# Gate's second half: one feature group of each pair of blocks by seven products of sums, and up's partial sums seeded in PSUM by ScalarE

## The chip, the cores and the metric

The kernel runs on one core of a Trainium2 chip. The metric is the device time of one execution in microseconds (us). TensorE (PE) does the matrix products, VectorE (DVE) and ScalarE (ACT) work on SBUF and PSUM, GpSimd (POOL) does little here, and SyncE (SP) issues nearly all DMA transfers.

## The reference

One transformer layer over 256 tokens with 2048 features, in float32: modulated input, a combined q/k/v projection, two kinds of attention over the tokens and 256 context tokens, an output projection, a gated residual and LayerNorm, and then a feed-forward part with the same residual rule. The change touches the feed-forward part alone:

```
def swiglu(u, w_gate, w_up, w_down):
    return (jax.nn.silu(u @ w_gate) * (u @ w_up)) @ w_down
```

Here u is 256 x 2048, w_gate and w_up are 2048 x 5632, and w_down is 5632 x 2048.

## The kernel before

**Precision by three products.** TensorE multiplies float32 rounded to a shorter form (F32R). Each operand is split into a rounded part hi and a remainder lo, and each product is three matmuls, hi x hi, hi x lo and lo x hi (`mm3`, L331 to L333). For the weights, ScalarE makes hi by a cast (L321) and VectorE lo by a subtraction (L322), on pieces of 128 x 1024 (`split_raw`). There are four buffers each for hi and lo (`HL_BUFS`), so the splits can run at most four pieces ahead of the matmuls, and four raw buffers of 1 MB (`RAW_BUFS`) into which SP loads the weights. For the tokens, u is turned (features on the partitions) and split once into `u2h` and `u2l` by `z_part`.

**Blocks and groups.** The 5632 columns of gate and up are cut into eleven blocks f of 512, the 2048 features into four groups g of 512 (four tiles k of 128 each). `project(accs, w_, f, g, ...)` loads and splits the weights of one group and one block and adds its product for both halves of the tokens (t = 0, 1) into two PSUM banks, 24 matmuls of 128x512 in all.

**Two halves.** Blocks 0 to 9 (`SPLIT_F` = 10) are worked in two halves, because the later features of u are ready late. The first half does one group (blocks 0 to 2) or two groups (blocks 3 to 9) and copies the sums to SBUF tiles `spills[f]` (gate in [0], up in [1]; L1568). The second half, a loop over f, does the remaining groups in new PSUM banks, and `activate` adds the spilled sums on VectorE (L1493, L1494), applies Silu on ScalarE (L1496) and multiplies (L1497). Block 10 is done whole.

**Turning.** The product h of a block is turned for the down projection: a 32x32 transpose on VectorE (`squares`, L1507), a trip through DRAM by SP's queue (`put`, `get`), and a split into `hTh` and `hTl` (`place`). `turn()` counts groups, and emits these steps some groups later.

**Order.** The attention part is put in order by a planner of the kernel's own. The feed-forward part is not: its instructions are ordered at compile time by a list scheduler, which keeps the program order as a priority, but puts an instruction earlier where its inputs are ready and its engine is free. At run time each engine follows that order.

**Banks and shared buffers.** PSUM has eight banks, four in a pool "acc" and four in a pool "wk". In SBUF, the tag "lgb" is one buffer, used by the sums of a modulation vector and then by `residual_base`, and "t2k" is four buffers, used by `z_part` and, from block 10 on, by the turning.

Of the kernel before, what the change touches and what calls it, by code (L numbers as in the profile page):

```python
# [13 lines left out]
F32 = mybir.dt.float32  # L14
F32R = mybir.dt.float32r
# [3 lines left out]
AF = mybir.ActivationFunctionType  # L19
ALU = mybir.AluOpType  # L20
# [27 lines left out]
SLACK = 2500  # L48
AHEAD = 14
EARLY_G = 2  # L50
ONE_F = 3
SPLIT_F = 10
LAG_S = 2
# [203 lines left out]
def dit_layer(ctx: ExitStack, tc: tile.TileContext, x, c, cx, c_ctx, w_ada, b_ada, w_in, q_norm_g,  # L257
# [68 lines left out]
    def split(hi, lo, src):  # L326
        nc.scalar.copy(hi, src)
        nc.vector.tensor_tensor(lo, src, hi.bitcast(F32), op=ALU.subtract)

    def mm3(ps, xh, xl, w, first, last, seeded=False):  # L330
        nc.tensor.matmul(ps, lhsT=xh, rhs=w[0], start=first, stop=False, skip_group_check=seeded)  # L331
        nc.tensor.matmul(ps, lhsT=xh, rhs=w[1], start=False, stop=False, skip_group_check=seeded)  # L332
        nc.tensor.matmul(ps, lhsT=xl, rhs=w[0], start=False, stop=last, skip_group_check=seeded)  # L333
# [1124 lines left out]
    def z_part(kk):  # L1458
        ps = wk_bank()
        for j in range(2):  # L1460
            for t in range(NT):
                nc.tensor.transpose(ps[:, (j * 2 + t) * P : (j * 2 + t + 1) * P],
                                    xt[:, t, (kk + j) * P : (kk + j + 1) * P], ident)
        uf = pb.tile([P, 2, SEQ], F32, tag="t2k", name="uf2", bufs=4)
# [4 lines left out]
        nc.vector.tensor_tensor(u2l[:, kk : kk + 2, :], uf, u2h[:, kk : kk + 2, :].bitcast(F32), op=ALU.subtract)  # L1469
# [12 lines left out]
    def project(accs, w_, f, g, first, last):  # L1482
        w = load_split(w_, g * 4, f * NB)
        for j in range(4):
            k = g * 4 + j
            for t in range(NT):
                mm3(accs[t], u2h[:, k, t * P : (t + 1) * P], u2l[:, k, t * P : (t + 1) * P], w[j], k == first, k == last)

    def activate(f, t, gate, up, hh):

        if f < SPLIT_F:
            sg, su = spills[f][0][:, t, :], spills[f][1][:, t, :]
            nc.vector.tensor_add(sg, sg, gate)  # L1493
            nc.vector.tensor_add(su, su, up)  # L1494
            gate, up = sg, su
        nc.scalar.activation(hh, gate, AF.Silu)  # L1496
        nc.vector.tensor_mul(hh, up, hh)  # L1497

# [28 lines left out]
    def flip_steps(f, gu):  # L1527

        if f < SPLIT_F:
            hh, hx = ([c[:, t, :] for t in range(NT)] for c in spills[f])  # L1530
        else:
            hh, hx = ([t2k(name) for t in range(NT)] for name in ("hh", "hx"))
        for t in range(NT):
            activate(f, t, gu[0][t], gu[1][t], hh[t])
# [87 lines left out]
    z_part(6)  # L1622
    cutoff = len(first_half) - 2
    run(merge(first_half[2 * ONE_F : cutoff], side))
    for kk in range(EARLY_G * 4, KD, 2):
        z_part(kk)
    run(first_half[cutoff:])
    flips = []

# [5 lines left out]
            flips.remove(e)  # L1635
            e[1]()

    for f in range(FFN // NB):
        if 5 <= f < 9:
            residual_base(f - 5)  # L1640
# [168 lines left out]
```

## Time and profile before

| | |
|---|---|
| median of 3 runs | 1134.47 us (1132.88 to 1136.02) |
| the profiled execution | 1133.72 us |
| its span, first to last instruction | 1131.9 us |
| PE, DVE, ACT busy, share of the span | 98%, 75%, 49% |
| granted TensorE clock | 0.996 |
| the feed-forward's second half, blocks 0 to 9 | about 585 to 835 us |

"Busy" is the time in which an engine has an instruction at work; matmuls overlap, so the distance between two starts is the better measure of TensorE. A line such as "L322 DVE TENSOR_TENSOR lo<-raw,hi" names the source line, the engine, the operation, what it writes and what it reads. In a list in order of time, the first number is the start in us, the second the duration (of a run of equal instructions where "x2" or more stands behind it), and the bracket is the idle time before it and what ended that. "PEld" is the loading of TensorE's stationary operand.

### The profile page before, as it was taken

How to read it: one execution, taken by the hardware profiler on the slowest of the kernel's cores; microseconds unless marked ns; L12 is line 12 of the kernel's file. 1: busy time of each engine (PE TensorE's matmuls, PEld its weight loads, DVE VectorE, ACT ScalarE, POOL GpSimd, SP SyncE). 2: the span in 40 equal slices, each digit the busy share in tenths (PEclk: the TensorE clock that was granted, in tenths of full speed). 3: DMA queues.
4: the chain of work that ended last, by engine and by line, in shares of the span. 5: the costliest groups of instructions: out<-in, count | busy, mean ns of one | idle time of the engine just before them, and what ended most of it. 6: DMA issues, size and time to landing. Idle time of an engine off the chain costs nothing.

```text
span 1131.9 us, 14059 instructions
## 1 busy us (share of the span) xinstructions
PE 1112.0 (98%) x5255; PEld 891.9 (79%) x5255; DVE 843.7 (75%) x1070; ACT 551.7 (49%) x795; POOL 43.2 (4%) x82
## 2 busy tenths in 40 slices
PE   8999999999999999999999999999999999999995
PEld 6767688778877787888888888888888888888884
DVE  5853489999999898777767566776766787686576
ACT  3341464878684255444464444444444344343442
POOL 1000050110200000010000000000000000000000
PEclk9999999999999999999999999999999999999998
DMA  9999999777999688999876776777677898887541
GB/s 316 395 389 354 405 362 359 250 253 225 362 339 385 241 301 308 343 312 317 303 234 216 240 237 223 230 242 258 213 265 241 272 370 303 312 303 260 187 148 74
DMA packets 178317, 321.26 MB, mean 284 GB/s; under 512 B 8732, under 2 KB 43196, under 8 KB 175943
## 3 DMA queue, kind: packets, MB, share of 16 engines
q1 hardware_dynamic: 177528, 320.03, 80.8%
q8 instruction: 41, 0.67, 0.2%
q10 hardware_dynamic: 720, 0.33, 0.1%
q14 instruction: 28, 0.23, 0.1%
HBM read 304.07 MB, written 16.25 MB: 283 GB/s over the span
## 4 chain that ended last, share of the span: by engine, by line
PE 79%; DMA 9%; DVE 7%; ACT 2%; issue 2%; SPq 1%; POOL 0%; ACTq 0%; DVEq 0%; POOLq 0%
PE acc L331 24%; PE acc L333 24%; PE acc L332 24%; DMA raw<-in_w_ada_dram 5%; PE wk L644 2%; DMA raw<-in_w_in_dram 1%; DVE adav L456 1%; PE wk L1071 1%; DVE g1b L456 1%; DVE lo L596 1%; DVE lo L322 1%; DMA pd<-hx 1%; DMA raw<-in_w_out_dram 1%; DMA pT<-pd 1%; PE wk L331 0%
## 5 line engine op out<-in xcount | busy, mean ns | idle before, releaser
L322 DVE TENSOR_TENSOR lo<-raw,hi 128x1024 fp32r<-128x1024 f32 x258 | 312.5, 1221 | 167.8 <-ACT hi L321 164.9
L321 ACT CAST hi<-raw 128x1024 fp32r<-128x1024 f32 x258 | 271.1, 1055 | 324.6 <-PE acc L333 295.0
L331 PE MATMUL acc<-hi,u2h 128*128 128x512 f32 x704 | 274.6, 390 | 1.4 <-ACT u2h L1583 1.4
L332 PE MATMUL acc<-lo,u2h 128*128 128x512 f32 x704 | 274.0, 389 | 0.7 <-DVE lo L322 0.7
L333 PE MATMUL acc<-hi,u2l 128*128 128x512 f32 x704 | 274.1, 389 | 0.0
L331 PEld LDWEIGHTS acc<-hi,u2h 128*128 128x128 f32 x704 | 132.1, 188 | 29.0 <-ACT u2h L1583 1.6
L332 PEld LDWEIGHTS acc<-lo,u2h 128*128 128x128 f32 x704 | 132.2, 188 | 28.4 <-DVE lo L322 1.1
L333 PEld LDWEIGHTS acc<-hi,u2l 128*128 128x128 f32 x704 | 132.1, 188 | 27.9 <-DVE u2l L1584 0.6
L593 ACT CAST hi<-raw 128x1024 fp32r<-128x1024 f32 (+1 forms) x86 | 87.2, 1030 | 111.4 <-DMA raw<-in_w_in_dram 56.9
L331 PE MATMUL acc<-hi,hTh 128*128 128x512 f32 x344 | 133.8, 389 | 0.4 <-ACT acc L1734 0.4
L332 PE MATMUL acc<-lo,hTh 128*128 128x512 f32 x344 | 133.9, 389 | 0.0
L333 PE MATMUL acc<-hi,hTl 128*128 128x512 f32 x344 | 133.9, 389 | 0.0
L456 DVE SCALAR_TENSOR_TENSOR adav<-raw,cs,adav 128x512 f32<-128x512 f32 (+1 forms) x128 | 121.3, 947 | 10.2 <-DMA raw<-in_w_ada_dram 8.4
L596 DVE TENSOR_TENSOR lo<-raw,hi 128x1024 fp32r<-128x1024 f32 (+1 forms) x86 | 101.3, 1192 | 13.9 <-ACT hi L593 13.5
L331 PE MATMUL acc<-hi,uh 128*128 128x512 f32 x256 | 104.0, 406 | 0.6 <-DVE qacc L829 0.3
L333 PE MATMUL acc<-hi,ul 128*128 128x512 f32 x256 | 100.2, 391 | 0.4 <-DVE ul L774 0.4
L332 PE MATMUL acc<-lo,uh 128*128 128x512 f32 x256 | 100.5, 392 | 0.0
L331 PEld LDWEIGHTS acc<-hi,hTh 128*128 128x128 f32 x344 | 64.6, 188 | 14.1 <-ACT acc L1734 0.8
L332 PEld LDWEIGHTS acc<-lo,hTh 128*128 128x128 f32 x344 | 64.6, 188 | 13.6 <-DVE lo L322 0.2
L333 PEld LDWEIGHTS acc<-hi,hTl 128*128 128x128 f32 x344 | 64.6, 188 | 13.4
L331 PEld LDWEIGHTS acc<-hi,uh 128*128 128x128 f32 x256 | 48.1, 188 | 19.6 <-issue 6.5
L333 PEld LDWEIGHTS acc<-hi,ul 128*128 128x128 f32 x256 | 48.1, 188 | 11.4 <-DVE ul L774 1.2
(224 smaller groups left out, 1149.2 us busy)
## 6 DMA issues: line engine op xcount, KB each, us to landing
raw<-in_w_ada_dram SPq DMA_DIRECT2D x70, 1024.0 KB, 8.6
raw<-in_w_gate_dram SPq DMA_DIRECT2D x44, 1024.0 KB, 5.9
raw<-in_w_up_dram SPq DMA_DIRECT2D x44, 1024.0 KB, 5.1
raw<-in_w_down_dram SPq DMA_DIRECT2D x44, 1024.0 KB, 5.0
raw<-in_w_ada_dram SPq DMA_DIRECT2D x48, 512.0 KB, 5.3
raw<-in_w_in_dram SPq DMA_DIRECT2D x18, 1024.0 KB, 10.2
raw<-in_w_out_dram SPq DMA_DIRECT2D x16, 1024.0 KB, 8.8
pd<-hx SPq DMA_DIRECT2D x64, 128.0 KB, 3.4
```

The lines of the kernel that those rows point to most:

```text
L321: nc.scalar.copy(hi[:, :n], raw[:, s : s + n])
L322: nc.vector.tensor_tensor(lo[:, :n], raw[:, s : s + n], hi[:, :n].bitcast(F32), op=ALU.subtract)
L331: nc.tensor.matmul(ps, lhsT=xh, rhs=w[0], start=first, stop=False, skip_group_check=seeded)
L332: nc.tensor.matmul(ps, lhsT=xh, rhs=w[1], start=False, stop=False, skip_group_check=seeded)
L333: nc.tensor.matmul(ps, lhsT=xl, rhs=w[0], start=False, stop=last, skip_group_check=seeded)
L456: nc.vector.scalar_tensor_tensor(a[:, c : c + piece], raw[:, f : f + piece], cs[:, 4 * (g * (G4 * NB // w) + j) + 2, None], a[:, c : c + p ...
L593: nc.scalar.copy(hl.hi[:, :n], raw.t[:, s : s + n])
L596: nc.vector.tensor_tensor(hl.lo[:, :n], raw.t[:, s : s + n], hl.hi[:, :n].bitcast(F32), op=ALU.subtract)
L644: nc.tensor.matmul(bank.t[32 * j : 32 * j + 32, :width], lhsT=cs[:, 4 * k + 2 - 2 * i : 4 * k + 34 - 2 * i], rhs=raw.t[:, c * width : (c + ...
L1071: nc.tensor.matmul(o_ps.t[:, : 2 * P].rearrange("p (g q) -> p g q", q=32), lhsT=v, rhs=pv[:, k], start=k == 0, stop=k == 3)
```

## The change

**Gate, group 2.** The second half takes the blocks in pairs (f0, f0 + 1). For group 2 (features k = 8 to 11) the gate's product of a pair is seen as a 2 x 2 by 2 x 2 product of submatrices: tokens in two halves t, features in two halves of two tiles, columns in the two blocks. That is eight products of submatrices; `folded` does it in seven (each two tiles, 6 matmuls), of which four use sums of tokens and four use sums of weights, with intermediate results shared between output banks:

- `token_forms` makes the four sums of tokens once, after `z_part` has put the features 8 to 11 in a tile `ufs` (tag "lgb"), splits them, and keeps them in the four "t2k" buffers.
- For each pair, VectorE makes four sums of weights in place in the raw buffers (128 x 1024 each), and each of the seven weight operands is split by a cast and a lo as other pieces are.
- A bank is started with a copy of another by ScalarE (`nc.scalar.copy(b, a)`, and so on), three copies a pair. The product numbered 1 goes to a bank e of its own and is added to the spilled sums of block f0 + 1 by VectorE.

Here the products are numbered as in the code: 11, 1, 12, 2, 3, 4, 22, in that order. The remaining groups of gate are added to the same banks by `project` with `seeded`.

**Up.** In blocks 2 to 9 ScalarE copies the spilled half sums into the PSUM banks before the products (`nc.scalar.copy(ups[t], su[t])`), so that the sum need not be added afterwards by VectorE. In blocks 0 and 1 the add stays. Up's banks come from the pool "wk". Gate's add and Silu stand behind its groups (`gated_half`), and both blocks' gates come ahead of both blocks' ups.

```
+    def token_forms(v):
+        v1, v2 = v[:, 0:2, :], v[:, 2:4, :]
+        a11, a21, a12, a22 = v1[:, :, :P], v1[:, :, P:], v2[:, :, :P], v2[:, :, P:]
+        tt = nc.vector.tensor_tensor
+        tt(a22, a21, a22, op=ALU.add)
+        tt(a21, a11, a21, op=ALU.subtract)
+        tt(a11, a22, a11, op=ALU.subtract)
+        tt(a12, a12, a11, op=ALU.subtract)
+        for n, (lr, x) in enumerate((((2, 3), v1), ((4, 1), v2))):
+            hi, lo = (pb.tile([P, 2, SEQ], F32R, tag="t2k", name=name, bufs=4) for name in ("fh", "fl"))
+            split(hi, lo, x)
...
+    def fold_products(ps, m, piece, first):
+        w = split_raw(piece)
+        for j in range(2):
+            mm3(ps, *forms[m][j], w[j], first and j == 0, j == 1, not first)
+
+    def folded(w_, f):
+        half = 2 * NB
+        r1, r2 = (load_raw(w_, FOLD_K, G4, (f + i) * NB, NB) for i in range(2))
+        b11, b21, b12, b22 = r1[:, :half], r1[:, half:], r2[:, :half], r2[:, half:]
+        a, e = wk_bank(), wk_bank()
+        b, c, d = (acc_bank() for _ in range(3))
+        tt = nc.vector.tensor_tensor
+        fold_products(a, 11, b11, True)
+        nc.scalar.copy(b, a)
+        tt(b11, b12, b11, op=ALU.subtract)
+        tt(b12, b22, b12, op=ALU.subtract)
+        fold_products(e, 1, b11, True)
+        tt(b11, b22, b11, op=ALU.subtract)
+        fold_products(a, 12, b21, False)
+        fold_products(b, 2, b11, False)
+        nc.scalar.copy(c, b)
+        tt(b21, b21, b11, op=ALU.subtract)
+        turn()
+        fold_products(c, 3, b12, False)
+        nc.scalar.copy(d, c)
+        fold_products(b, 4, b22, False)
+        fold_products(c, 22, b21, False)
+        for t in range(NT):
+            sg = spills[f + 1][0][:, t, :]
+            tt(sg, sg, e, op=ALU.add)
+        turn()
+        return (a, c), (b, d)
+
+    def gated_half(f, t, gate):
+        hh = spills[f][0][:, t, :]
+        nc.vector.tensor_add(hh, hh, gate)
+        nc.scalar.activation(hh, hh, AF.Silu)
...
+    ufs = pb.tile([P, 4, SEQ], F32, tag="lgb", name="ufs")
+    for i, kk in enumerate(range(EARLY_G * 4, KD, 2)):
+        z_part(kk, ufs[:, 2 * i : 2 * i + 2, :] if kk < FOLD_K + 4 else None)
+    token_forms(ufs)
     run(first_half[cutoff:])
...
+    for f0 in range(0, SPLIT_F, 2):
...
+        gates = folded(w_gate, f0)
+        for i, f in enumerate((f0, f0 + 1)):
+            for g in range(groups[f], ng):
+                if g * 4 != FOLD_K:
+                    project(gates[i], w_gate, f, g, None, KD - 1, True)
+                    turn()
+            for t in range(NT):
+                gated_half(f, t, gates[i][t])
+        for i, f in enumerate((f0, f0 + 1)):
+            ups = [wk_bank() for _ in range(NT)]
+            su = [spills[f][1][:, t, :] for t in range(NT)]
+            for t in range(NT):
+                if f0:
+                    nc.scalar.copy(ups[t], su[t])
+            for g in range(groups[f], ng):
+                project(ups, w_up, f, g, groups[f] * 4, KD - 1, f0 > 0)
+                turn()
+            if not f0:
+                for t in range(NT):
+                    nc.vector.tensor_add(su[t], su[t], ups[t])
+                ups = su
+            flips += flip_steps(f, (None, ups))
```

More of the change, by code (lines that the diff above doesn't have):

```diff
@@ L50 @@
 EARLY_G = 2
+FOLD_K = 8
 ONE_F = 3
@@ L1456, in dit_layer, with z_part @@
     hTl = [pb.tile([P, 4, SEQ], F32R, tag=f"hTl{f}", name="hTl") if f < KF // 4 - SPLIT_F else None for f in range(KF // 4)]
-    def z_part(kk):
+    def z_part(kk, uf=None):
         ps = wk_bank()
@@ L1463, in z_part @@
                                     xt[:, t, (kk + j) * P : (kk + j + 1) * P], ident)
-        uf = pb.tile([P, 2, SEQ], F32, tag="t2k", name="uf2", bufs=4)
+        if uf is None:
+            uf = pb.tile([P, 2, SEQ], F32, tag="t2k", name="uf2", bufs=4)
         for j in range(2):
@@ L1480, in residual_base, with project @@
             nc.vector.scalar_tensor_tensor(xt[:, t, sl], lb, ALPHA, xt[:, t, sl], op0=ALU.mult, op1=ALU.add)
-    def project(accs, w_, f, g, first, last):
+    def project(accs, w_, f, g, first, last, seeded=False):
         w = load_split(w_, g * 4, f * NB)
@@ L1486, in project @@
             for t in range(NT):
[L1487 to L1497, printed above, removed]
+                mm3(accs[t], u2h[:, k, t * P : (t + 1) * P], u2l[:, k, t * P : (t + 1) * P], w[j],
+                    k == first and not seeded, k == last, seeded)
@@ new lines, in dit_layer @@
+    forms = {}
+    def token_forms(v):
[9 more added lines that the diff above has]
+            split(hi, lo, x)
+            for i, m in enumerate(lr):
+                forms[m] = [(hi[:, j, i * P : (i + 1) * P], lo[:, j, i * P : (i + 1) * P]) for j in range(2)]
+        for m, (t, k) in {11: (0, FOLD_K), 12: (0, FOLD_K + 2), 22: (1, FOLD_K + 2)}.items():
+            forms[m] = [tuple(u[:, k + j, t * P : (t + 1) * P] for u in (u2h, u2l)) for j in range(2)]
@@ L1533, in flip_steps @@
         for t in range(NT):
-            activate(f, t, gu[0][t], gu[1][t], hh[t])
+            if f >= SPLIT_F:
+                nc.scalar.activation(hh[t], gu[0][t], AF.Silu)
+            nc.vector.tensor_mul(hh[t], gu[1][t], hh[t])
             squares(hh[t], hx[t])
@@ L1636, in turn @@
             e[1]()
-    for f in range(FFN // NB):
-        if 5 <= f < 9:
-            residual_base(f - 5)
+    for f0 in range(0, SPLIT_F, 2):
+        for f in (f0, f0 + 1):
+            if 5 <= f < 9:
+                residual_base(f - 5)
+        gates = folded(w_gate, f0)
[20 more added lines that the diff above has]
+            flips += flip_steps(f, (None, ups))
+    for f in range(SPLIT_F, FFN // NB):
         gu = []
```

2 lines of the change are left out of this document (removed).

## The prediction

> **What bounds the kernel now.** I read the head of the page first, then the windows, the chain, and the waits of the one stage that the change touches, and last the order of instructions where one block ends.
>
> ```profile
> span 1131.9 us, 14059 instructions
> PE 1112.0 (98%) x5255; PEld 891.9 (79%) x5255; DVE 843.7 (75%) x1070; ACT 551.7 (49%) x795; POOL 43.2 (4%) x82
> ```
>
> Shares over the whole span say little about one stage. The feed-forward's second half (blocks 0 to 9, feature groups 1 to 3 or 2 to 3) lies at about 585 to 835 us; a window of that length inside it (times, PE, PEld, DVE, ACT, POOL busy, clock, DMA share, GB/s), the chain and the waits of that window:
>
> ```profile
> 588.00:838.00 250.00, 250.00 (x1104) 207.02 (x1103) 170.92 (x195) 118.04 (x131) 0.00 (x0) 1.00 0.72 236
> ```
>
> ```profile
> by line: PE acc L333 33.4%; PE acc L332 33.4%; PE acc L331 33.3%
> ```
>
> ```profile
> ACT hi L321 <- PE acc L333: 118.7, 77, 1.7
> DVE lo L322 <- ACT hi L321: 74.3, 60, 1.5
> ```
>
> TensorE is the chain, without a gap: 250.00/1104 = 0.2264 us a matmul, at full clock. Nobody it waits for appears; the others wait for it. ScalarE's cast waits until TensorE frees one of the four hi/lo buffers, VectorE's lo waits for the cast. A piece (one buffer, 1024 columns) is 12 matmuls here, 2.72 us, so the splits run three pieces or 8.2 us ahead. VectorE is 68% busy (170.92/250), DMA 0.72. So only two things can change the time: the number of matmuls, and new gaps on TensorE.
>
> **Gain.** Per pair of blocks the gate's group 2 is 2 blocks x 4 k x 2 t x 3 = 48 matmuls in 4 pieces. The seven products have 2 j x 3 = 6 each: 42, in seven pieces. Five pairs save 30 x 0.2264 = 6.79 us (0.6%). No other matmul goes. A product puts 6 matmuls in a row into one bank, where a group alternates between two. The first products of block 0 put 12 into one; of these, the first and last of nine:
>
> ```profile
> 393.68 0.40 PE L331 MATMUL acc<-hi,u2h 128*128 128x512 f32 x1
> 395.51 0.39 PE L333 MATMUL acc<-hi,u2l 128*128 128x512 f32 x1
> ```
>
> 1.83/8 = 0.229 us apart: I add nothing for it.
>
> **What the fold costs VectorE and ScalarE.** Prices:
>
> ```profile
> L322 DVE TENSOR_TENSOR lo<-raw,hi 128x1024 fp32r<-128x1024 f32 x258 | 312.5, 1221 | 167.8 <-ACT hi L321 164.9
> L321 ACT CAST hi<-raw 128x1024 fp32r<-128x1024 f32 x258 | 271.1, 1055 | 324.6 <-PE acc L333 295.0
> ```
>
> ```profile
> L1568 ACT COPY spill<-acc x36: 576/587/591, 411.9 to 585.3; 128x512 f32<-128x512 f32 x36
> L1493 DVE TENSOR_TENSOR spill<-spill,acc x20: 680/680/683, 603.5 to 824.7; 128x512 f32<-128x512 f32 x20
> L1494 DVE TENSOR_TENSOR spill<-spill,acc x20: 680/681/683, 617.4 to 835.6; 128x512 f32<-128x512 f32 x20
> ```
>
> and what they come to back to back, around the end of block 4 (start, duration):
>
> ```profile
> 703.34 1.23 DVE L322 TENSOR_TENSOR lo<-raw,hi 128x1024 fp32r<-128x1024 f32 x1 [1.49 <-ACT hi L321]
> 704.49 1.28 DVE L1494 TENSOR_TENSOR spill<-spill,acc 128x512 f32<-128x512 f32 x2
> 705.68 1.29 DVE L1497 TENSOR_TENSOR spill<-spill 128x512 f32<-128x512 f32 x2
> 706.89 1.29 DVE L1507 STREAM_TRANSPOSE spill<-spill 128x512 f32<-128x512 f32 x2
> 708.11 2.32 DVE L322 TENSOR_TENSOR lo<-raw,hi 128x1024 fp32r<-128x1024 f32 x2
> ```
>
> 703.34 to 704.49 is 1.15 for a 1024-wide operation, 704.49 to 705.68 is 0.60 for each 512-wide one. Added per pair on VectorE: 3 more lo (3.4) and 4 sums of weights, for which the nearest row is the lo of the same size (4.6), and 2 adds of the fifth product (1.2). Removed: up's adds in eight of ten blocks, 2 each, 2.4 a pair. Net +6.8 of some 42 us a pair: VectorE goes from 68 to about 85%, still below TensorE on average. ScalarE gets 3 more casts (3.1), 3 PSUM-to-PSUM copies (1.8) and 4 seeds of up (2.4), from 47 to some 64%. So nothing is bound by a total; what counts is the fold itself, 42 x 0.2264 = 9.5 us of TensorE, in which VectorE must do 11 wide and 2 narrow operations, 13.9 us. The lead pays for the difference, if it is enough.
>
> **The chain in the fold.** The third bank is seeded by a copy of the second, and this is the row of a copy that TensorE waits for. The first two lines give matmul to copy, the others copy to matmul:
>
> ```profile
> 584.15 0.39 PE L333 MATMUL acc<-hi,u2l 128*128 128x512 f32 x1
> 584.57 1.27 ACT L1568 COPY spill<-acc 128x512 f32<-128x512 f32 x2 [0.98 <-PE acc L333]
> ...
> 1103.57 0.39 PE L333 MATMUL acc<-hi,hTl 128*128 128x512 f32 x1
> 1103.71 0.59 ACT L1734 COPY acc<-xt 128x512 f32<-128x512 f32 x1
> ...
> 1104.35 0.50 PE L331 MATMUL acc<-hi,hTh 128*128 128x512 f32 x1 [0.40 <-ACT acc L1734]
> 1104.69 0.39 PE L332 MATMUL acc<-lo,hTh 128*128 128x512 f32 x1
> ```
>
> From the last matmul's start 0.42 to the copy, 0.64 from copy to matmul: 1.06 in place of 0.23, and the first matmul after it takes 0.34 in place of 0.23: 0.95 us lost. Which copies are exposed? The first (a to b) runs under product 1, 1.36 us long. The second (b to c) is not covered: product 3 follows product 2 at once, and all that is left (3, 4, 22) needs this copy or comes later. The third (c to d) could lie under product 4 only if that came first, but 4 goes into b, needs no d, and does come first after 3: covered. So one exposed copy a pair, 5 x 0.95 = 4.75.
>
> Timetable of a fold, zero where TensorE starts product 11, the block before having just ended. VectorE reaches zero having done lo 11, two sums, lo 1, a sum and lo 12 (buffers came free at -8.2, -5.4, -2.7). Then: last sum to 1.0; mul and transpose of the block before, four at 0.60, to 3.4 (above, they too go before the waiting lo); lo 2 to 4.55. TensorE wants it at 4.08+0.23: late by about 0.25. Product 2 ends near 5.7, copy, product 3 at 6.5; lo 3, 4, 22 end at 5.7, 6.8, 8.0, each ahead of its product (6.5, 7.9, 9.3). Lo of the next group ends at 10.3, its product starts at 10.6. So 5 x 0.25 = 1.3 more. Blocks 0 and 1 keep up's adds on VectorE; block 1's two lie just before the second fold and push lo 2 by 1.2, once.
>
> **The rest.** The seeds of up take banks that have long been free, and the adds they replace waited for nobody: zero; if ScalarE were full, each would delay a cast by 0.59, against a lead of 8 us. Gate's add and Silu stand where they did: zero. The loads:
>
> ```profile
> raw<-in_w_gate_dram SPq DMA_DIRECT2D x44, 1024.0 KB, 5.9
> ```
>
> They are as many; the pair's two raw buffers are given back at some 7 and 8 us after zero rather than one after the other, so the next two loads land at 13 and 14, where the first cast from them comes due at 13.5 and its matmuls 8 us later: zero. What SP holds behind them are the puts of turned blocks, which only the down projection reads: zero. The forms of the tokens (4 operations of 256, 2 casts, 2 lo, some 4 us) stand ahead of the first fold, where before has
>
> ```profile
> 572.40 1.91 PE L1462 MATMUL wk<-ident,xt 128*128 128x128 f32 x16
> ...
> 577.96 1.29 DVE L1469 TENSOR_TENSOR u2l<-uf,u2h 128x512 fp32r<-128x512 f32 x2
> ...
> 582.53 1.06 ACT L321 CAST hi<-raw 128x1024 fp32r<-128x1024 f32 x1 [0.77 <-PE acc L333]
> ```
>
> The second of the two parts needed is through at 578.6, so the forms at about 583; product 1 comes at 586.5. ScalarE has caught up with its casts at 582.5, where it waits for TensorE again. Zero, at worst 3 once, if the buffer that the forms share with the residual's constants goes to the latter first.
>
> **Sum.** -6.79 + 4.75 + 1.3 + 1.2 = +0.5 us on the profiled execution's 1133.72 (span 1131.9 and 1.8 around it). That lies 0.75 below the median of the runs, so 1134.47 + 0.5 = 1135.0. One step is 0.3%, 3.4 us: about what a measurement of this kernel tells from no change. Unknown prices: a copy from PSUM to PSUM has no row; between 0.59 (both other directions) and 1.2 (read and write not overlapped) it is 0 to 3 in all; I take 0.59. A lo that is in time takes 2.5 off; TensorE with no gap at all gives -6.8.
>
> **Rivals.**
>
> *The gaps get filled or are shorter.* Instructions are put in order at compile time, not as written (the rows of the third rival show it). If a group's matmuls into bank a came ahead into the copy's gap, or lo 2 before the mul, the loss per pair falls below 0.68 us: -3.4 to -6.8, 1127.7 to 1131. Against it: those matmuls need a fifth buffer, freed by product 2 itself. Chance 0.20.
>
> *VectorE's queue is late in the fold (slower).* The timetable has it busy without a break from -1 to 10 us, ScalarE nearly so. Two narrow operations more ahead of lo 2 (a place, the fifth product's adds) cost 1.2 a pair; a cast just started before the copy b to c costs up to 1.0. Both in all folds: +11, 1146. It decides above 2.0 us lost a pair, 6.8/5 + 3.4/5; my sum has 1.45. For it: the order is fixed beforehand, by durations that need not be these. Chance 0.34.
>
> *Copies hold the casts.* If ScalarE took each copy ahead of the next cast, cast and lo would start only when TensorE already waits: 0.2 + 0.6 + 1.1 + 1.2 = 3.1 lost at each of three copies, 46 us, about 1174. The Trainium skill, "PSUM — Partial Sum Buffer", section "Engine vs sequencer instructions", says that ScalarE's queue is strictly first in, first out, so by that rule a waiting copy would hold all behind it. The order of before speaks against so bad a one:
>
> ```profile
> 569.87 1.05 ACT L321 CAST hi<-raw 128x1024 fp32r<-128x1024 f32 x1 [2.08 <-PE acc L333]
> 571.91 1.27 ACT L1568 COPY spill<-acc 128x512 f32<-128x512 f32 x2 [0.98 <-PE acc L333]
> ```
>
> A block's copies to spill are written ahead of the next block's casts, and yet this cast of the next block is through before them. Chance 0.03.
>
> *The clock drops.* The window behind the gap at 1104 us:
>
> ```profile
> 1104.00:1110.00 6.00, 5.65 (x25) 4.68 (x26) 3.83 (x5) 1.87 (x3) 0.00 (x0) 1.00 0.00 0
> ```
>
> The granted clock is 1.00, and the pitch was back within one matmul. Were the 18 matmuls behind each gap at half speed all the same, it would be 4.1 a pair, +21, 1155. The Trainium skill, "TensorE: Matmul & The Clock Gate", section "HAM oscillation — how this bites in real kernels", sets the limit at idle gaps above 3.4 us; by that rule nothing changes, and the trace agrees (0.8 us, 1.00). Its section "A second HAM failure mode: psum-queue depth-cycling" tells of short idles that throttle too; no row here shows that. Chance 0.01.
>
> **Numbers.** Forecast (within 3.4 us) 0.42, filled 0.20, late 0.34, the other two 0.04: faster 0.20, same 0.42, slower 0.38. The range from 1129 to 1147 leaves out the last microsecond of the filled case (0.04) and the tail of the late one with the two others (0.14). The likeliest case alone: 1131 to 1138.
>
> **What would show it.** TensorE in 585 to 828: 30 matmuls fewer, and five gaps of about 0.8 us that end with a copy into a bank, five shorter ones that end with lo. VectorE's share there near 85%, lo's waits for the cast much shorter. Wrong if TensorE waits for lo more than 1 us in a fold, if it waits for the copies a to b or c to d, if the first fold waits for the forms, or if a load is late behind the fold.

## The result, and the profile after

The changed kernel takes 1141.62 us (median of 4 runs, 1140.04 to 1143.16), the kernel before 1134.93 in the same comparison: a ratio of 1.0065 with the interval 1.0044 to 1.0086, so slower by some 0.65%, or 7 us. The profiled execution took 1141.75 us with a span of 1140.0, against 1133.72 and 1131.9 before. The head of the page of the changed kernel:

```profile
span 1140.0 us, 14118 instructions
PE 1109.0 (97%) x5225; PEld 887.0 (78%) x5225; DVE 883.6 (78%) x1105; ACT 582.0 (51%) x843; POOL 43.8 (4%) x82
```

The 30 matmuls are gone (5255 to 5225), and still the span is 8.1 us longer. The window inside the second half that the prediction used (times, PE, PEld, DVE, ACT, POOL busy, clock, DMA share, GB/s), in the changed kernel:

```profile
588.00:838.00 250.00, 241.49 (x1043) 197.41 (x1043) 208.00 (x226) 144.11 (x174) 0.00 (x0) 0.99 0.69 231
```

TensorE, which had no idle microsecond here before, now has 8.5 of them; VectorE is at 83% (208.00/250), and the clock is no longer exactly 1.00. What TensorE waits for between 560 and 860 us in the changed kernel (engine and line, the line waited for, us in total, times, longest):

```profile
PE acc L332 <- ACT acc L1533: 5.5, 5, 1.3
PE acc L332 <- ACT hi L322: 2.3, 1, 2.3
PE acc L333 <- DVE lo L323: 0.7, 1, 0.7
PE wk L333 <- DVE lo L323: 0.4, 1, 0.4
```

In the changed kernel all lines from the helpers on stand one lower: L322 is the cast, L323 the lo, L332 to L334 the matmuls. L1526, L1533 and L1537 are the copies a to b, b to c and c to d. L1527, L1528, L1530 and L1534 are the four sums of weights, L1542 product 1's adds, L1717 up's adds in blocks 0 and 1, L1588 and L1559 a block's multiplication and transpose, L1481 and L1482 the residual's operations. So the copy b to c is waited for five times, as the prediction has it, the copies a to b and c to d never, and each of the other waits occurs once.

The five folds side by side are the key to the rest. For each, "lost" is the time that TensorE took beyond its matmuls at 0.2266 us each, added up from the starts of consecutive matmuls, from this fold's first matmul to the next fold's. Seven products in place of eight save 6 matmuls, 1.36 us, so a fold that loses 1.36 breaks even.

| fold, starts at | 585.65 | 655.29 | 712.57 | 756.24 | 799.90 | sum | against 6.80 saved |
|---|---|---|---|---|---|---|---|
| lost, us | 5.72 | 4.26 | 1.51 | 1.53 | 1.52 | 14.54 | +7.7 |

That is nearly the whole result: the profiled executions differ by 8.0 us. Three folds are alike and lose about what they save; the first two lose 4.2 and 2.7 us more.

**A steady fold.** The fifth one, in order of time (start, duration, in the bracket the idle time before and what ended it):

```profile
805.09 1.04 ACT L322 CAST hi<-raw 128x1024 fp32r<-128x1024 f32 x1
805.12 0.39 PE L334 MATMUL acc<-hi,fl 128*128 128x512 f32 x1
806.04 0.58 ACT L1533 COPY acc<-acc 128x512 f32<-128x512 f32 x1
806.67 0.50 PE L332 MATMUL acc<-hi,fh 128*128 128x512 f32 x1 [1.17 <-ACT acc L1533]
807.01 0.40 PE L333 MATMUL acc<-lo,fh 128*128 128x512 f32 x1
```

Product 2's last matmul starts at 805.12. The copy could have followed 0.42 later, at 805.54, but a cast that had started at 805.09 was on ScalarE, and the copy runs at 806.04. Start to start the two matmuls around it are 1.55 apart instead of 0.23, and the next one adds 0.11: 1.44 us, where the prediction had 0.95. The copy itself, which had no row before, takes 0.58, at the low end of its bounds. lo 2, for which 0.25 was forecast, isn't waited for at all.

**The second fold.** VectorE before lo 2, then TensorE:

```profile
655.63 1.28 DVE L1717 TENSOR_TENSOR spill<-spill,wk 128x512 f32<-128x512 f32 x2
656.83 1.29 DVE L1588 TENSOR_TENSOR spill<-spill 128x512 f32<-128x512 f32 x2
658.03 1.30 DVE L1559 STREAM_TRANSPOSE spill<-spill 128x512 f32<-128x512 f32 x2
659.25 1.18 DVE L323 TENSOR_TENSOR lo<-raw,hi 128x1024 fp32r<-128x1024 f32 x1
660.49 0.50 PE L333 MATMUL acc<-lo,fh 128*128 128x512 f32 x1 [0.74 <-DVE lo L323]
663.27 0.80 PE L332 MATMUL acc<-hi,fh 128*128 128x512 f32 x1 [1.34 <-ACT acc L1533]
```

Block 1's adds stand just ahead of lo 2, as forecast, and cost 1.0 us. But after the second gap something is new: a matmul of 0.80 us where the steady fold has 0.50.

**The first fold.** VectorE is later still:

```profile
585.44 1.05 ACT L322 CAST hi<-raw 128x1024 fp32r<-128x1024 f32 x1 [3.00 <-DVE raw L1527]
588.71 0.69 DVE L1481 SCALAR_TENSOR_TENSOR xt<-xt,lgb 128x512 f32<-128x512 f32 x1 [0.95 <-DMA lgb<-in_ln_g_dram]
589.32 1.22 DVE L1530 TENSOR_TENSOR raw<-raw 128x1024 f32<-128x1024 f32 x1
590.62 2.94 ACT L322 CAST hi<-raw 128x1024 fp32r<-128x1024 f32 x3 [1.72 <-DVE raw L1530]
591.72 0.80 PE L332 MATMUL acc<-hi,fh 128*128 128x512 f32 x1 [2.26 <-ACT hi L322]
592.31 0.63 PE L333 MATMUL wk<-lo,u2h 128*128 128x512 f32 x1
592.74 0.63 PE L334 MATMUL wk<-hi,u2l 128*128 128x512 f32 x1
```

The sum L1530 (the operand of product 2) was to be done before the fold begins at 585.65. It runs at 589.32, 3.7 us late. Part of that is an idle time of 0.95 us in front of an operation of `residual_base` (L1481) whose constants are still on their way by DMA, and the operation itself, 0.6; the rest was there before, because the first of the sums (L1527) only starts at 584.14, behind the splits of the forms. ScalarE's cast waits for the sum, TensorE for the cast. After that the matmuls are 0.43 us apart (592.31, 592.74), not 0.227. The windows of the granted clock behind the two gaps (same columns as above):

```profile
591.00:594.00 3.00, 2.28 (x5) 1.83 (x6) 3.00 (x4) 2.56 (x3) 0.00 (x0) 0.60 0.00 0
664.00:668.00 4.00, 4.00 (x14) 3.18 (x13) 3.51 (x5) 1.83 (x4) 0.00 (x0) 0.67 0.69 226
```

TensorE's clock goes to half for some 3.4 us in each, eight matmuls that cost 0.2 us more each: about 1.6 us in either fold, 3.2 of the 7.7 lost.

### The profile page after: what moved, and what is told of

Same layout as the page of the kernel before. It is cut to its first block, busy times and chain, and to the rows that moved or that the text cites. A ratio compares the mean times of both kernels' runs of the same rounds, so it can differ in the third digit from the quotient of the medians.

```text
span 1140.0 us, 14118 instructions
## 1 busy us (share of the span) xinstructions
PE 1109.0 (97%) x5225; PEld 887.0 (78%) x5225; DVE 883.6 (78%) x1105; ACT 582.0 (51%) x843; POOL 43.8 (4%) x82
## 4 chain that ended last, share of the span: by engine, by line
PE 80%; DVE 7%; DMA 6%; ACT 4%; issue 2%; SPq 1%; POOL 0%; ACTq 0%; DVEq 0%; POOLq 0%
PE acc L332 21%; PE acc L333 20%; PE acc L334 20%; PE wk L334 4%; PE wk L333 4%; PE wk L332 4%; DMA raw<-in_w_ada_dram 2%; PE wk L645 2%; DVE lo L323 2%; ACT hi L322 2%; PE wk L1072 2%; DMA raw<-in_w_out_dram 1%; DVE adav L457 1%; DMA pd<-hx 1%; DMA raw<-in_w_down_dram 1%
## 5 line engine op out<-in xcount | busy, mean ns | idle before, releaser
L322 ACT CAST hi<-raw 128x1024 fp32r<-128x1024 f32 x273 | 285.6, 1054 | 299.9 <-PE acc L334 204.4
L323 DVE TENSOR_TENSOR lo<-raw,hi 128x1024 fp32r<-128x1024 f32 x273 | 329.4, 1221 | 129.7 <-ACT hi L322 125.6
L332 PE MATMUL acc<-hi,u2h 128*128 128x512 f32 x422 | 164.9, 391 | 1.4 <-ACT u2h L1637 1.4
L333 PE MATMUL acc<-lo,u2h 128*128 128x512 f32 x422 | 164.3, 389 | 0.7 <-DVE lo L323 0.7
L334 PE MATMUL acc<-hi,u2l 128*128 128x512 f32 x422 | 164.4, 390 | 0.0
L334 PE MATMUL acc<-hi,hTl 128*128 128x512 f32 x344 | 133.7, 389 | 0.0
L332 PE MATMUL acc<-hi,hTh 128*128 128x512 f32 x344 | 133.1, 389 | 0.4 <-ACT acc L1815 0.4
L332 PE MATMUL acc<-hi,uh 128*128 128x512 f32 x256 | 103.8, 405 | 0.5 <-ACT kvacc L828 0.2
L334 PE MATMUL acc<-hi,ul 128*128 128x512 f32 x256 | 100.1, 391 | 0.3 <-DVE ul L775 0.3
L332 PEld LDWEIGHTS acc<-hi,u2h 128*128 128x128 f32 x422 | 79.2, 188 | 18.0 <-ACT u2h L1637 1.6
L333 PEld LDWEIGHTS acc<-lo,u2h 128*128 128x128 f32 x422 | 79.2, 188 | 17.3 <-DVE lo L323 1.1
L334 PEld LDWEIGHTS acc<-hi,u2l 128*128 128x128 f32 x422 | 79.2, 188 | 17.0 <-DVE u2l L1638 0.6
L333 PE MATMUL wk<-lo,u2h 128*128 128x512 f32 x232 | 90.7, 391 | 0.0
L334 PE MATMUL wk<-hi,u2l 128*128 128x512 f32 x232 | 90.7, 391 | 0.0
L332 PE MATMUL wk<-hi,u2h 128*128 128x512 f32 x232 | 90.5, 390 | 0.0
L332 PEld LDWEIGHTS acc<-hi,hTh 128*128 128x128 f32 x344 | 64.6, 188 | 14.2 <-ACT acc L1815 0.8
L333 PEld LDWEIGHTS acc<-lo,hTh 128*128 128x128 f32 x344 | 64.6, 188 | 13.9 <-DVE lo L323 0.5
```

What stands on the lines that cost most here:

```text
L322: nc.scalar.copy(hi[:, :n], raw[:, s : s + n])
L323: nc.vector.tensor_tensor(lo[:, :n], raw[:, s : s + n], hi[:, :n].bitcast(F32), op=ALU.subtract)
```

## The experiments

Each was compared with the kernel before on the same chip. Edits are shown against the changed kernel unless the text says otherwise, and only their deciding lines; the kernel before had medians of 1132.3 to 1133.3 us in these comparisons. The account that they test: steady folds break even, and the loss is what stands in VectorE's queue ahead of the first two folds, with the clock's drop on top of it. Each expectation names its own theories. The table has the microseconds lost in each fold and behind it up to the next, for the kernels that have all five folds and no matmuls added:

| kernel | 1 | 2 | 3 | 4 | 5 | ratio to before (interval) |
|---|---|---|---|---|---|---|
| changed kernel | 5.72 | 4.26 | 1.51 | 1.53 | 1.52 | 1.0065 (1.0044 to 1.0086) |
| up's adds on VectorE | 5.14 | 2.73 | 3.15 | 3.14 | 3.14 | 1.0116 (1.009 to 1.0141) |
| product 2 before 12 | 5.93 | 3.09 | 1.36 | 1.36 | 1.34 | 1.0061 (1.0043 to 1.008) |
| two sums on GpSimd, own buffer | 7.04 | 6.34 | 3.38 | 3.47 | 5.01 | 1.0192 (1.0167 to 1.0216) |
| two sums on GpSimd | 6.80 | 5.39 | 4.90 | 4.98 | 3.48 | 1.016 (1.0141 to 1.0179) |
| a buffer of its own for the forms | 7.64 | 2.68 | 1.49 | 1.49 | 1.48 | 1.0077 (1.0059 to 1.0095) |
| forms early | 5.98 | 2.71 | 1.48 | 1.48 | 1.48 | 1.0061 (1.0044 to 1.0079) |
| and block 1 seeded | 3.33 | 1.48 | 1.48 | 1.48 | 1.48 | 1.0046 (1.0028 to 1.0064) |
| and order, mul later | 3.11 | 1.45 | 1.00 | 1.76 | 1.31 | 1.0028 (1.0013 to 1.0043) |
| residual late | 1.29 | 1.48 | 1.52 | 1.49 | 9.78 | 1.0074 (1.0058 to 1.009) |

**1. Folds from block 4 on.** Blocks 0 to 3 are done in eight products again, through `project`, but up's seeds stay.

```
-        gates = folded(w_gate, f0)
+        gates = folded(w_gate, f0) if f0 >= 4 else None
```

> Blocks 0 to 3 take gate's group 2 as eight products, only the pairs from block 4 on are folded. Theory A (the loss sits in the first two folds, 15.2 and 13.8 us, the other three take 11.0 against 10.9 for eight products): +0.5 us on before, so within 0.3% of it, about 1135.4, and no window with a lower granted clock. Theory B (every fold costs alike, 6.7/5 = 1.3 us): three folds, +4.0, about 1139.

Measured: 1134.04 us, 1.0013 (1.0001 to 1.0025). The three folds lose 1.48, 1.52 and 1.52, so without the first two nearly the whole loss is gone, and theory B's 4.0 us lie outside the interval (at most 2.8). What is left is outside of them: with the residual's constants arriving where the first fold would be, two lo's come late and TensorE loses 2.2 us. VectorE and TensorE of this kernel:

```profile
608.90 1.29 DVE L1481 SCALAR_TENSOR_TENSOR xt<-xt,lgb 128x512 f32<-128x512 f32 x2 [1.87 <-DMA lgb<-in_ln_g_dram]
...
613.83 0.50 PE L333 MATMUL acc<-lo,u2h 128*128 128x512 f32 x1 [1.04 <-DVE lo L323]
```

**2. The fold without up's seeds.** Up's adds go back to VectorE in all blocks.

```
+SEED_UP = False
-                if f0:
+                if SEED_UP and f0:
                     nc.scalar.copy(ups[t], su[t])
...
-            if not f0:
+            if not (SEED_UP and f0):
```

> The folds without up's seeds: the adds of up stay on VectorE in all blocks. Theory A (the second fold was longer because the adds of block 1 stand before it in VectorE's queue): folds 3, 4 and 5 become like the second, 13.8 in place of 11.0, +2.7 each, +8 on the changed kernel, about 1150. Theory B (the adds wait for nobody and nobody for them): no change, about 1141.6.

Measured: 1145.9 us, 1.0116. The folds 3 to 5 lose 3.14 in place of 1.52. Lines stand one lower still; the third fold:

```profile
712.76 0.50 PE L334 MATMUL wk<-lo,u2h 128*128 128x512 f32 x1 [1.15 <-DVE lo L324]
716.67 0.50 PE L333 MATMUL acc<-hi,fh 128*128 128x512 f32 x1 [1.34 <-ACT acc L1534]
```

A lo is 1.15 us late because two adds (1.2 us) stand before it. So the adds are on the path of a fold: they cost 1.6 us each time (3.14 for 1.52), where the prediction priced the adds of a pair at 1.2 and the expectation had 2.7, and the seeds are what makes a steady fold break even. In the profiled execution (1141.98, clock 0.997) no fold has a half clock: not the second, although its gaps are 0.74 and 1.35 us as in the changed kernel, and not the first, with a gap of 2.10; the slower ones of its runs have a mean clock of 0.992 to 0.994 (1144.93 to 1148.74 us).

**3. Seeds and the order by pairs, without the fold.**

```
-    token_forms(ufs)
...
-        gates = folded(w_gate, f0)
+        gates = None
```

The gate's groups then all go through `project`, as before, and the forms are not made.

> Up's seeds and the order by pairs alone, all of gate by eight products. Theory A: no step of this is on TensorE's path, within 0.3% of before, about 1135. Rival (the seeds hold up ScalarE's casts, or up waits for them): 16 seeds at up to 0.6, +3 to +7, 1138 to 1142.

Measured: 1132.52 us, 0.9997 (0.9985 to 1.001). TensorE waits for nothing between 560 and 860 us. The seeds and the order are free, and worth nothing by themselves.

**4. Product 2 ahead of product 12.** Then the copy b to c has product 12, 1.36 us, to run under.

```
-        fold_products(a, 12, b21, False)
         fold_products(b, 2, b11, False)
         nc.scalar.copy(c, b)
+        fold_products(a, 12, b21, False)
```

> Product 2 is written ahead of product 12, so that 12 (1.36 us) can run while ScalarE copies the second bank to the third. Theory A (that copy, with a cast ahead of it, is the whole gap of the steady folds, 1.3 us): -1.3 in each of five folds at best, 1135; -2 where lo 12, now later, takes part of it. Theory B (VectorE is the limit in the fold and the gap only moves to a lo): about 1141.6, with the gap in front of product 12 or 22.

Measured: 1139.03 us, 1.0061. The wait for the copy b to c is gone from all five folds (in the second, the copy a to b is waited for instead, 0.34 us), and a steady fold still loses 1.36 where it lost 1.52. The third fold of this kernel:

```profile
718.12 0.50 PE L333 MATMUL acc<-lo,fh 128*128 128x512 f32 x1 [0.37 <-DVE lo L323]
...
721.12 1.09 PE L332 MATMUL acc<-hi,u2h 128*128 128x512 f32 x3
722.04 0.40 PE L333 MATMUL wk<-lo,u2h 128*128 128x512 f32 x1
```

Now lo is late, inside the fold and again just behind it. (The row with x3 holds three matmuls, so the gap behind it is 0.92 - 0.68 = 0.24 us; where an expectation below speaks of 0.9 us there, it seems to have taken the row for one matmul.) The gap has moved from ScalarE to VectorE: the copy was covering for VectorE, which has 13.9 us of work in a fold of 9.5 by the prediction's sum.

**5 and 6. Two of the sums on GpSimd**, with the order of experiment 4; the first of the two kernels also gives the forms a buffer of their own (as experiment 7).

```
-        tt(b12, b22, b12, op=ALU.subtract)
+        nc.gpsimd.tensor_tensor(b12, b22, b12, op=ALU.subtract)
...
-        tt(b21, b21, b11, op=ALU.subtract)
+        nc.gpsimd.tensor_tensor(b21, b21, b11, op=ALU.subtract)
```

> All five folds, with three edits together: product 2 ahead of 12, two of the four sums of weights (the second and the last) on GpSimd, and the features of the forms in a buffer that the residual's constants do not use. Theory A (VectorE's queue is the limit): folds of 9.8 to 10.4 us in place of 10.9 for eight products, the first some 13; -2 to -4 on before, 1129 to 1131. Rival (GpSimd's sums are slow, over 4 us, or slow VectorE's down): 1135 to 1141.

> Product 2 ahead of 12, and the second and last sums of weights on GpSimd; otherwise the changed kernel. Theory A (once the copy is covered, VectorE's queue is what is late): the waits for lo in and behind the steady folds (0.5 and 0.9 us in the run with the order alone) go, -1.2 in each of three folds and more in the second, 1133 to 1136. Rival: GpSimd's sum takes over 4 us or makes VectorE's operations longer, the wait moves to product 22's cast, 1139 or more.

Measured: 1153.39 us, 1.0192 (1.0167 to 1.0216), and 1151.56 us, 1.016: the worst of all, far from the 1129 to 1131 and 1133 to 1136 that were expected. GpSimd and VectorE just ahead of the third fold of the second kernel:

```profile
711.54 2.40 POOL L1528 TENSOR_TENSOR raw<-raw 128x1024 f32<-128x1024 f32 x1 [43.66 <-DVE raw L1527]
712.60 2.42 DVE L323 TENSOR_TENSOR lo<-raw,hi 128x1024 fp32r<-128x1024 f32 x1 [1.20 <-ACT hi L322]
```

The sum takes 2.40 us in place of 1.22, and the lo beside it, 1.22 otherwise, takes 2.42: it ends at 715.02, 1.08 behind the end of GpSimd's sum (713.94), as if it had begun only then. What is taken off VectorE, 1.22, comes back in the lo, 1.20. The Trainium skill, "SBUF — State Buffer", section "Who interferes with whom", says that a VectorE instruction with two inputs in SBUF contends with a GpSimd instruction that reads SBUF, and that the order of issue decides which of the two is blocked; these two rows agree.

**7. A buffer of its own for the forms**, so that the residual's constants don't wait for it.

```
-    ufs = pb.tile([P, 4, SEQ], F32, tag="lgb", name="ufs")
+    ufs = main.tile([P, 4, SEQ], F32, tag="adav", name="ufs")
```

> The changed kernel with the features of the forms in a buffer that the residual's constants do not use. Theory A (in the first fold VectorE's queue stood behind an operation of the residual whose constants were loaded late, because the buffer was taken): the residual's operations go back to where before had them, the first fold loses 1.6 to 3 us less and its clock need not drop, 1137 to 1140. Rival (the forms themselves use up the lead): no change within 1 us, 1141.

Measured: 1142.01 us, 1.0077. The first fold does not get better (7.64): without the wait for the DMA the residual's operations are there earlier and take their place in the queue among the sums, and the clock is at half for 6.8 us in place of 3.4 (some 2.8 of the 7.64, for 1.6 of the 5.72). The shared buffer alone is not the cause.

**8. Matmuls to fill the gaps.** Matmuls whose result is not used go into the gaps of the first two folds (10 and 5, 3 and 5), into banks that are started anew afterwards. They do nothing but keep TensorE busy.

```
+        for i in range(n):
+            nc.tensor.matmul(into, lhsT=forms[m][1][0], rhs=w[1][0], start=True, stop=True)
...
-        fold_products(e, 1, b11, True)
+        fold_products(e, 1, b11, True, c, 10 if f == 0 else 3 if f == 2 else 0)
...
-        fold_products(b, 2, b11, False)
+        fold_products(b, 2, b11, False, d, 5 if f < 4 else 0)
```

> The changed kernel with TensorE kept at work in the gaps of the first two folds: matmuls into a bank that is overwritten afterwards, 10 and 5 in the first fold, 3 and 5 in the second (their results are not used). Theory A (the half clock after those gaps is due to the gaps): granted clock 1.00 in all windows of both folds, some 1.6 us less in each, 1138.4. Rival (the clock drops for another reason, or the filler only lengthens the folds): 1141 or more, with windows below 0.9.

Measured: 1138.19 us, 1.0048 (1.0032 to 1.0063), with runs from 1137.68 to 1139.15. The windows behind the gaps in this kernel:

```profile
591.00:594.00 3.00, 2.92 (x13) 1.98 (x12) 3.00 (x4) 2.35 (x3) 0.00 (x0) 1.00 0.00 0
664.00:668.00 4.00, 4.00 (x20) 3.30 (x19) 4.00 (x6) 3.69 (x5) 0.00 (x0) 1.00 0.88 283
```

The clock stays at 1.00 in this execution, and the kernel with 23 matmuls that do nothing is some 2 us faster (1.0065 to 1.0048, though the intervals overlap). One trace would not prove that the half clock follows from the gaps, since experiment 2 has such gaps without it; the count over all traces in the last section bears it out. With the fillers counted as lost, the first fold loses 5.1 and the second 2.7. The second gains all of the clock's 1.6; the first gains only 0.6, because its 15 fillers take 3.4 us and the two gaps that they fill were 2.26 and 0.66. What remains is mostly VectorE's lateness by itself.

**9. Forms early.** The tokens' sums and splits are made right behind group 2's modulation, at about 510 us, with buffers of their own (for which some scratch tiles move to other buffers).

```
+    def early_forms():
+        ufs = main.tile([P, 4, SEQ], F32, tag="adav", name="ufs")
+        for i in range(2):
+            z_part(FOLD_K + 2 * i, ufs[:, 2 * i : 2 * i + 2, :])
+        token_forms(ufs)
+
+    side = second_modulation(2, late_sums[0]) + [early_forms] + second_modulation(3, late_sums[1])
```

> The changed kernel with the forms of the tokens made some 70 us earlier, right after the modulation of their features (which needs other buffers for some scratch tiles). Theory A (the forms take VectorE in the stretch in which the first fold's lead would be built): the first fold goes from 15.2 to 11 to 12.5 us and its clock stays up, -3 to -4 on the changed kernel, ratio to before about 1.003. Rival (the first fold is long for another reason, such as the copies of the last sums to SBUF): 15 us still, 1.006.

Measured: 1140.59 us, 1.0061, the first fold still at 5.98. VectorE around it shows why:

```profile
584.87 1.22 DVE L1527 TENSOR_TENSOR raw<-raw 128x1024 f32<-128x1024 f32 x1
586.01 0.68 DVE L1481 SCALAR_TENSOR_TENSOR xt<-xt,lgb 128x512 f32<-128x512 f32 x1
586.61 1.22 DVE L1528 TENSOR_TENSOR raw<-raw 128x1024 f32<-128x1024 f32 x1
```

The residual's operations now lie between the sums. Without the clock's share, which is larger here (some 2.8 us), the first fold loses 3.2 in place of 4.1: moving the forms did help, by about 0.9, and the clock hid it.

**10. And block 1 seeded.** To experiment 9, block 1's up is seeded too (`if f:` in place of `if f0:`), which takes its two adds off VectorE.

> As the run with the forms early, and up's sums of block 1 are put in PSUM by ScalarE too, so that no adds of up stand before the second fold. Theory A (those two adds, 1.2 us, make lo 2 late, and the gap that follows the half clock): all five folds take 11.0 to 11.5, 55 to 57 us against 54.4 for the eight products: +1 to +2, ratio 1.001 to 1.002. Rival: the second fold stays at 12 to 14 us, 1.003.

Measured: 1137.83 us, 1.0046, more than either theory had. The second fold is now like the others (1.48): block 1's adds and the half clock that followed them were all that it lost more. The first one still loses 3.33. On VectorE and ScalarE ahead of it:

```profile
577.63 0.69 DVE L1481 SCALAR_TENSOR_TENSOR xt<-xt,lgb 128x512 f32<-128x512 f32 x1 [1.53 <-DMA lgb<-in_ln_g_dram]
...
583.02 2.00 ACT L322 CAST hi<-raw 128x1024 fp32r<-128x1024 f32 x2 [4.78 <-DVE raw L1527]
```

**11. And order, mul later.** To experiment 10, the order of experiment 4, and the multiplication and turning of a pair's second block written behind the next fold.

```
         gates = folded(w_gate, f0)
+        if f0:
+            flips += flip_steps(held[0], (None, held[1]))
```

> As the run before, with product 2 ahead of 12, and the mul and transposes of a pair's second block written behind the next pair's fold. Theory A (with the copy covered, VectorE's 2.4 us of mul and transposes are what makes the los in and behind the fold late): folds of 9.6 to 10.4 and no gap behind them, -2 to -6 on before, ratio 0.995 to 0.998. Rival (the ring of four buffers, or ScalarE's casts, hold the fold at 10.6 and the group behind it): 0.999 to 1.002.

Measured: 1137.52 us, 1.0028 (1.0013 to 1.0043), the fastest with all five folds, and still slower than before, where 0.995 to 0.998 was expected. Inside the folds 2 to 5 only 0.4 to 0.6 us is lost; behind them lo is late and takes the rest, 1.00 to 1.76 together. The work taken out of the fold is missing just behind it. The profiled execution lasted 1138.39, some 3 us more than its folds account for. They lie outside the folds: the first fold starts at 587.15, where the kernel before starts the same matmul at 585.05, and the last 1000 matmuls take 228.2 us in place of 227.3.

**12. Residual late.** To experiment 10: the residual's constants get buffers that come free only after the last fold, so that its operations cannot run before.

```
-        lgb = pb.tile([P, 2, NB], F32, tag="lgb", name="lgb")
-        lg, lb = lgb[:, 0, :], lgb[:, 1, :]
+        lg, lb = t2k("lgb"), t2k("lgb")
```

> As the run with the forms early and block 1 seeded, and the residual's constants go into the four buffers that the forms hold until the last fold, so that none of the residual's operations on VectorE (nor its wait for their transfer) can stand in the first fold. Theory A (the first fold was late by two things in VectorE's queue, the forms and the residual): all five folds take 10.9 to 11.5 us, 55 to 56 us against 54.4, granted clock 1.00 throughout, +0.6 to +2 on before, ratio 1.0005 to 1.002. Rival (the first fold is long for a third reason): it stays at 12.8 us or more, ratio 1.003 to 1.005. If the residual is late for the down projection, it shows after 860 us.

Measured: 1140.75 us, 1.0074, but for another reason: folds 1 to 4 lose 1.29 to 1.52, so all of them now about break even, the first included. There TensorE has one wait left, for the copy:

```profile
PE acc L332 <- ACT acc L1532: 0.7, 1, 0.7
```

What the kernel loses lies behind the fifth, where all of the residual's operations come at once. VectorE, then TensorE (the residual's lines are L1480 and L1481 here):

```profile
812.26 1.29 DVE L1481 SCALAR_TENSOR_TENSOR xt<-lgb,xt 128x512 f32<-128x512 f32 x2
813.47 1.29 DVE L1480 SCALAR_TENSOR_TENSOR xt<-xt,lgb 128x512 f32<-128x512 f32 x2
814.67 1.29 DVE L1481 SCALAR_TENSOR_TENSOR xt<-lgb,xt 128x512 f32<-128x512 f32 x2
...
817.07 4.63 DVE L323 TENSOR_TENSOR lo<-raw,hi 128x1024 fp32r<-128x1024 f32 x4
...
818.35 0.80 PE L333 MATMUL wk<-lo,u2h 128*128 128x512 f32 x1 [5.56 <-DVE lo L323]
```

A gap of 5.56 us and a stretch at half clock behind it: 8.3 of the 9.78 us. Taking these 8.3 off 1140.75 leaves 1132.4, the time of before (1132.3). So the first fold's loss can be taken apart step by step, roughly: 1.6 by the clock, 0.9 by the forms (experiment 9), 2.0 by the residual (3.33 in experiment 10 to 1.29 here), and 1.3 that remain. The residual was taken away only with the forms already early, so how the two act together is not shown. The second fold's extra loss is block 1's adds and the clock behind them, and with none of these the fold is worth nothing either way.

## Why the prediction was right and wrong

The range, 1129 to 1147, holds the time; the likeliest case, no change at 1135.0, is not what happened. It was the slower case: "VectorE's queue is late in the fold" (0.34), with a piece of "the clock drops" (0.01). That the range holds is little proof, for it is 18 us wide and holds gains and losses alike. The late case is met on average, 14.54/5 = 2.9 us a pair against its limit of 2.0, but not in the way that it tells: three folds lose 1.5, and VectorE was late in the first two alone.

- **Gain: right.** 30 matmuls fewer, 6.8 us, pitch unchanged by the new order of banks.
- **The copy b to c: right place, a third too small.** One exposed copy a pair and no other, as worked out. 0.95 was the price of a copy that begins when its matmul is through; a cast on ScalarE made it 1.44 in the steady folds. The late case named just that, "a cast just started before the copy b to c costs up to 1.0"; it cost 0.5 a fold, 1.5 us over the three.
- **lo 2: too large where all is steady.** 0.25 a pair was forecast, 0 was measured in folds 3 to 5. Steady folds together: 1.20 forecast, 1.52 measured, with 1.36 as break-even. The core of the sum held.
- **Block 1's adds: right**, 1.2 forecast and 1.0 measured for the wait. That the gap behind it, 1.4 us of work later, would be followed by half clock was not foreseen: 1.6.
- **The forms at "Zero, at worst 3 once": the step that failed.** The forms were looked at by when they would end (583 forecast; VectorE's last one starts at 583.53), not by what they take from VectorE's lead. The timetable let VectorE enter each fold with the sums of products 1 and 2 already made, in the first fold too; there it had made one of them (L1527 at 584.14). And one engine's queue was left out: the residual's operations on VectorE, which wait for a DMA and hold all that is behind them. The trace of before has them in the same place, with the same wait (VectorE of the kernel before, L1479 there):

```profile
591.22 1.29 DVE L1479 SCALAR_TENSOR_TENSOR xt<-xt,lgb 128x512 f32<-128x512 f32 x2 [0.93 <-DMA lgb<-in_ln_g_dram]
```

  There TensorE waited for nothing, because the splits were some 8 us ahead by the prediction's count; the prediction does not mention the row. In the changed kernel the first fold loses 5.72, 4.2 more than a steady one, 1.6 of that by the clock. Experiments 9 and 12 put some 0.9 of it on the forms and 2.0 on the residual.
- **"The clock drops", 0.01: too sure.** The evidence was one gap of 0.4 us idle (the 0.8 in the prediction is from start to start) with the clock at 1.00, and a rule. By the Trainium skill, "TensorE: Matmul & The Clock Gate", section "HAM oscillation — how this bites in real kernels", it takes an idle gap of more than 3.4 us. Here it went to half after 2.26 us, and after 0.74 and 1.34 with 1.4 us of work between: the measurement decides, and gaps shorter than that limit do throttle. A single gap of 1.17 us every 43 us did not, in any profiled fold. The last section shows what told the cases apart.
- **Seeds, loads, copies a to b and c to d: right**, all at zero (experiment 3, and the list of waits).
- **The signs named beforehand:** five gaps that end with the copy b to c came, idle for 0.66 to 1.34 us. Gaps that end with lo came in two folds and not in five; in the changed kernel none of them reached 1 us, and no load was waited for. The first fold waited for the forms only by way of VectorE's queue.
- **VectorE's share:** about 85% forecast, 83% measured. It was the right number to compute, and the wrong one to rely on: in 9.5 us of fold it has 13.9 us of work, and what counts is how far ahead it comes in.

Still open: the medians of some kernels lie 2 to 3 us above what the folds of their profiled execution give (experiment 10: 1134.97 profiled, 1137.83 median). These runs have a lower mean clock (0.994 to 0.996, profiled 0.997), which fits more stretches of half clock in them; but only one execution of each kernel has a trace. Another source is the time ahead of the folds: the program's 2000th matmul, before which none of these kernels has a fold, starts between 387.3 and 391.7 us in the traces.

## What to carry to other kernels

When TensorE is without gaps, saving matmuls by sums of operands pays only if the engine that makes the sums is ahead at that place: cost the burst against the lead, not the share of the whole span, and do it for the first instance by itself, with everything else that is in that queue at the time. Any wait on a DMA in an in-order queue counts against all that stands behind it. And a gap on TensorE should be priced at more than its length: where gaps left six matmuls or fewer in 3.4 us, in which 15 fit, the clock cost 1.6 us more, and up to 2.8 where it stayed down for 6.8 us.

## What the runs showed of the hardware that was not expected

- TensorE's clock goes to half (0.43 us a matmul instead of 0.227) for stretches of 3.4 or 6.8 us, and the length of a gap does not decide it. Gaps of 0.74 and 1.34 us brought it in the second fold of the changed kernel, gaps of 0.74 and 1.35 in that of experiment 2 did not. What the traces show is a grid: within each of the fourteen, the granted clock changes only at times that lie whole multiples of 3.413 us apart. If the time from 560 to 870 us of all traces is cut into stretches on this grid, 15 matmuls start in one at the full rate. Of 18 stretches in which at most six start, 17 are followed by a stretch at half clock; of 1255 in which seven or more start, none is. So the two gaps drop the clock where they fall into one stretch, and not where they fall into two. The second fold on its grid, in the changed kernel and then in experiment 2 (the number behind PE's busy time counts matmuls at work):

```profile
659.85:663.26 3.41, 1.43 (x5) 0.86 (x5) 3.41 (x4) 2.78 (x6) 0.00 (x0) 1.00 0.44 121
663.26:666.67 3.41, 3.40 (x8) 2.73 (x9) 3.41 (x5) 1.36 (x2) 0.00 (x0) 0.50 0.39 103
...
656.24:659.65 3.41, 2.18 (x9) 1.15 (x7) 3.41 (x4) 2.09 (x4) 0.00 (x0) 1.00 0.43 115
659.65:663.06 3.41, 2.56 (x11) 2.11 (x12) 3.41 (x5) 2.62 (x5) 0.00 (x0) 1.00 0.29 50
663.06:666.47 3.41, 3.41 (x17) 2.82 (x16) 3.41 (x4) 2.69 (x3) 0.00 (x0) 1.00 0.98 374
```

  In experiment 8 the fillers leave no stretch with fewer than eight. Experiments 9 and 10 lie at the edge: they have nearly the same first fold (idle 0.40, 1.24 and 0.66; 0.52, 1.24 and 0.66) and six matmuls in the emptiest stretch, and only the former drops. The limit is counted from these traces, not explained by them.

- A copy by ScalarE from one PSUM bank to another costs what the other directions cost: 0.58 us for 128x512, against 0.59.
- VectorE's subtraction of 128x1024 beside a GpSimd sum of the same size: 2.42 us instead of 1.22.
